# Hybrid attention and DeltaNet layer: gates projected last, two inverse groups in the merge stage, one PSUM bank for both scan chains

## The chip, the cores and the metric

One core of a Trainium2 chip runs the whole layer in one launch. The metric is the device time of that launch in microseconds (us), lower being better. TensorE (PE) multiplies matrices into PSUM, whose eight banks are shared out by the kernel; VectorE (DVE), ScalarE (ACT) and GpSimd (POOL) do the rest; SyncE (SP) issues most of the transfers.

## The reference

One layer over 1024 latent tokens of width 1024, with 256 context tokens. The mixer has two halves of width 512, fed by one input projection: neighbourhood attention with 8 heads, and a gated DeltaNet that runs over the sequence in both directions with 4 heads of 128. Each half is multiplied by a SiLU gate, and one output projection follows.

```python
na_q, na_k, na_v, na_z, g_qkv, g_z, g_b, g_a = jnp.split(h @ w_in, IN_SPLITS, axis=-1)
...
o_na = neighborhood_attention(heads(na_q), heads(na_k), heads(na_v),
                              heads(na_kc), heads(na_vc), rpb)
...
# DeltaNet, for each head and direction, over chunks of tokens
t_inv = lax.linalg.triangular_solve(eye + a, jnp.broadcast_to(eye, a.shape),
                                    left_side=True, lower=True, unit_diagonal=True)
...
def step(state, xs):
    v_new = u_n - jnp.einsum('bhcd,bhde->bhce', w_n, state)
    o_n = (jnp.einsum('bhcd,bhde->bhce', q_n, state)
           + jnp.einsum('bhij,bhje->bhie', qk_n, v_new))
    state = state * gl_n[..., None, None] + jnp.einsum('bhcd,bhce->bhde', k_n, v_new)
    return state, o_n
...
y = jnp.concatenate([o_na * jax.nn.silu(na_z), o_g * jax.nn.silu(g_z)], axis=-1) @ w_out
x = x + gate[:, None] * rmsnorm(y, g_post)
```

## The kernel before

The code names the work; a scheduler that lays it out on a modelled timeline, by priorities that the code can raise, sets the order on each engine. Engines then run their lists strictly in order, and wait on semaphores. Products that need precision are made of three matmuls, of a high and a low part.

- **Phases 0 and 2** (to about 454 us). The input is normalized into hh and hl (high and low part, latent) and chh and chl (context). For each DeltaNet head h, phase 2 runs steps named by a letter each: Q, K, V are convolutions, T and B turn queries and keys, F is `delta_front`, which makes the triangular matrices `pm` of head h - 1 and stores them. A step p takes one piece from `projections`, a generator of independent matmuls: gates (`pz`), attention's queries and keys (`pq`, `pk`), values.
- **Inverses.** Each 128-row block of `pm` is inverted in two parts. First its 32-row diagonal blocks, 320 in all, in three groups of 120, 120 and 80 partitions (`inv_groups`): the blocks are gathered in `ab_dram`, loaded as `ab`, and DVE solves them in 31 pairs of a multiply (into `tb`) and a subtract (into `vb`). The result is stored as `yd`. Groups 0 and 1 run in phase 2, group 2 in phase a2.
- **Phase a2** (about 454 to 554 us). `inv_merge`, once a head, joins the small inverses into the 128-row ones: it loads `vd` (from `yd`) and `pmf` (from `pm_dram`), transposes `vd` to `ld` on DVE, and goes in four rounds of products and evictions (tz, tu at 32 rows, tz2, tu2 at 64 rows) to `tm`, stored in `tm_dram`. What `projections` has left is laid between.
- **Phase b** (from about 554 us). Attention goes through 64 units (4 pairs of heads, 8 row tiles, 2 heads), each with products pc, pl and po. Beside it runs `delta_scan`, head by head: ten steps of two directions d = 0 and 1, each with three matmuls in a row into the bank of that direction (`pa`), read in turn by DVE (y), ACT (vn) and DVE (s, the state), and two more products into `pos`. `phase4` then makes the output products `py`, in seven and then eight banks; the last scan results go into their last piece.

The eight banks of phase b before: two for pc, two for pl, one for po, one for each direction's pa, one for pos.

Of the kernel before, what the change touches and what calls it, by code (L numbers as in the profile page):

```python
# [11 lines left out]
F32 = mybir.dt.float32  # L12
F32R = mybir.dt.float32r
# [7 lines left out]
P = 128  # L21
# [118 lines left out]
class K:  # L140
# [50 lines left out]
    def phase0(self):  # L191
# [4 lines left out]
        self.chh = self.hp.tile([P, KC, CT], F32R, name="chh")  # L196
        self.chl = self.hp.tile([P, KC, CT], F32R, name="chl")
# [330 lines left out]
    def na_proj(self, ap, ps, pairs):  # L528
        for p in pairs:
            for i in range(2):  # L530
                w = self.load_w(self.wp, 512 * i + P * p, P, f"n{'qk'[i]}{p}")
                for gr in (2, 0, 1)[1 - i:]:
                    pq = ps.tile([P, 512], F32, name=f"p{'qk'[i]}{p}_{gr}", tag="pj", bufs=3)
                    self.mm_qk(pq, w, i, gr)
                    self.qk_out(p, i, gr, pq)
                    yield
            yield from self.gate_proj(ap, ps, p, 1536 + P * p)
# [47 lines left out]
    def na_attn(self, na, ps):  # L585
# [10 lines left out]
        nxt = load(0)  # L596
        for p in range(4):
# [65 lines left out]
    def na_unit(self, ps, p, rt, ct, qk, vv, gts, mk, sums, po):  # L663
# [7 lines left out]
        for hh in range(2):  # L671
# [7 lines left out]
            pl = ps.tile([P, 512], F32, name=f"pl{p}_{u}_{hh}", tag="sl", bufs=2)  # L679
# [39 lines left out]
    def phase2(self):  # L719
        tc, nc, I = self.tc, self.nc, self.I  # L720
        ps = self.ps
        with tc.tile_pool(name="cv", bufs=1, side="right", reuse_waits="tile") as cv:
# [4 lines left out]
            self.fill, self.ready = self.projections(cv), []  # L727
# [31 lines left out]
            blocks = iter(())  # L759
            for h in range(4):  # L760
                for c in "QK":
                    step(h, c)
                    next(blocks, None)
                for _ in blocks:
                    pass
                step(h - 1, "F") if h else step(h, "G")
                if h > 1:
                    blocks = self.inv_groups((h - 2,), lambda nm, n: cv.tile([P, n], F32, name=nm, tag=nm[:2]))
                for c in "RVppTppUB":
                    step(h, c)  # L770
                    next(blocks, None)
# [6 lines left out]
    def projections(self, pool):  # L778
        for h in range(1, 4):
            yield from self.gate_proj(pool, self.ps, 4 + h, 3584 + P * h)  # L780
        yield from self.na_proj(pool, self.ps, [1])
        w = self.load_w(self.wp, [(1024, 264)], 264, "nv0", halves=4)
        for t in range(2, 12, 2):
            self.values(pool, w, 0, [t % 10, t % 10 + 1])
            yield
        self.ready.append(True)
        yield from self.na_proj(pool, self.ps, [2, 3])
# [226 lines left out]
    def inv_merge(self, g3, ps, h):  # L1014
        nc = self.nc
        pm = []
        for d in range(2):
            pool, tag = (g3, f"pm{d}") if h % 2 else (self.pf, f"kk{d}")
            pm.append(pool.tile([P, 10, P], F32, name=f"pmf{h}_{d}", tag=tag))
            nc.sync.dma_start(pm[d], self.pm_dram[h][:, d])  # L1020
        vd = g3.tile([P, 2, 10, 32], F32, name=f"vd{h}", tag="vd", bufs=2)
# [5 lines left out]
        tm = [g3.tile([P, 10, P], F32, name=f"tm{h}_{d}", tag="tm", bufs=3) for d in range(2)]  # L1027
# [7 lines left out]
        for b in range(4):  # L1035
            sl = slice(32 * b, 32 * b + 32)
            cp = nc.scalar.copy
            cp(tm[0][sl, :, sl], vd[sl, 0])
            cp(tm[1][sl, :, sl], ld[sl, 1])
            cs = slice(32 * (b % 2), 32 * (b % 2) + 32)  # L1040
            nc.scalar.copy(xo[sl, :, cs], ld[sl, 0] if b < 2 else vd[sl, 1])
        zt = g3.tile([P, 2, 10, 32], F32, name=f"zt{h}", tag="zt", bufs=1)
        for d in range(2):
            pz = ps.tile([P, 10, 32], F32, name=f"tz{h}_{d}", tag="ta", bufs=3)
            for t in range(10):
                for b in (0, 2):
                    s1, s2 = slice(32 * b, 32 * b + 32), slice(32 * b + 32, 32 * b + 64)
                    nc.tensor.matmul(pz[s2, t, :], pm[d][s1, t, s2], ld[s1, d, t, :], start=True, stop=True,
                                     tile_position=(32 * b, 32 * b + 32))
            for b in (0, 2):  # L1050
                s2 = slice(32 * b + 32, 32 * b + 64)
                nc.scalar.copy(zt[s2, d], pz[s2])
        yield
# [18 lines left out]
        for d, t0, n in parts:  # L1072
            pz = ps.tile([P, 8, 64], F32, name=f"tz2{h}_{d}{t0}", tag="ta", bufs=3)
# [18 lines left out]
    def delta_scan(self, g3, ps, h):  # L1092
# [23 lines left out]
        chain = [ps.tile([P, 512], F32, name=f"pa{h}_{d}", tag=f"pa{d}", bufs=1)[:, :P] for d in range(2)]  # L1116
# [75 lines left out]
    def phase4(self, p4, ps, last):  # L1192
# [17 lines left out]
        banks = {"sc": 2, "sl": 2, "po": 1, "pa0": 1, "pa1": 1, "os": 1}  # L1210
# [65 lines left out]
    def phase_a2(self):  # L1276
        tc, ps = self.tc, self.ps
        with tc.tile_pool(name="a2", bufs=1, side="right", reuse_waits="tile") as ap:
            ready = self.ready
            buf = lambda nm, tag, n: self.pf.tile([P, n], F32, name=f"{nm}_{tag}", tag=tag)  # L1280

            def blocks():
                vv = buf("ab", "vv", 2 * S)
                yield from self.inv_groups((2,), lambda nm, n: buf("tb2", "qh0", n) if n < S else vv[:, :S] if "ab" in nm
                                           else vv[:, S:])
                self.mk = self.pf.tile([P, MTOT], mybir.dt.bfloat16, name="mk")
                self.load(self.mk, self.I["masks"])
                while len(ready) < 4:
                    yield
                self.na_pairs = {0: self.na_load(None, 0)}  # L1290
                yield

            def merges():
                for h in range(4):
# [3 lines left out]
                    ready.append(h)  # L1298
                    yield

            pr, gens = self.fill, (blocks(), merges())
            credit = [0.0, 0.0]
            first = True
            for _ in range(3):
                next(pr)
            for _ in pr:
                for i, (g, r) in enumerate(zip(gens, (3, 3))):
                    credit[i] += r
                    while credit[i] > 0:
                        if i:  # L1310
                            with tc.high_priority(offset=200):
                                next(g, None)
                        elif first:
                            first = False
                            with tc.high_priority(offset=300):
                                next(g, None)
                        else:
                            next(g, None)
                        credit[i] -= 1
            for g in gens:  # L1320
                for _ in g:
                    pass
# [24 lines left out]
    def run(self):  # L1347
        tc = self.tc
        with ExitStack() as ctx:
# [12 lines left out]
            with tc.tile_pool(name="np", bufs=1, side="right", reuse_waits="tile") as self.np, ExitStack() as fx:  # L1362
                with tc.tile_pool(name="wp", bufs=1, side="left", reuse_waits="tile") as self.wp, \
                     tc.tile_pool(name="hp", bufs=1, side="left", reuse_waits="tile") as self.hp, \
                     tc.tile_pool(name="as", bufs=1, space=PSUM, reuse_waits="tile") as self.ps:
                    with tc.tile_pool(name="vp", bufs=1, side="right", reuse_waits="tile") as self.vp:
                        self.phase0()
                    self.phase2()
# [25 lines left out]
```

## Time and profile before

| | |
|---|---|
| Median of three runs | 905.87 us (905.06 to 906.93) |
| Profiled execution, its own time | 904.01 us |
| Its span | 902.3 us |
| Mean granted TensorE clock | 0.963 |
| Matmuls on TensorE | 6082 |

The profile is of one execution; its own time is 1.7 us more than the span that the profile shows, and 1.9 us less than the median. A row of a timeline gives start, duration, engine, line, operation, output<-input, a count where several are joined, and in brackets the idle time before it with what ended it. A row of a table by stage gives the stretch, its length, and for each engine the busy time with the number of instructions, then the granted TensorE clock, the share of DMA busy, and GB/s.

### The profile page before, as it was taken

Reading aid. Unit: us, or ns where it says so; the run is one execution under the profiler, and the core shown is the slowest. Engines: PE = TensorE matmul, PEld = TensorE weight load, DVE = VectorE, ACT = ScalarE, POOL = GpSimd, SP = SyncE. Lnnn points to the kernel's source line nnn. Section 1 sums busy time; section 2 is a strip of 40 time slices with the busy share of each in tenths; the row PEclk is TensorE's granted clock in tenths of the full one; section 3 lists DMA queues with packets and bytes.
Section 4 is the critical chain, followed back from the end, with each engine's and each line's share of the span. In section 5 each row is a group of like instructions: output and inputs, shape, how many; then the busy total and the mean of one; then the engine's idle time right before and its main releaser. Section 6 shows DMA issues by size and latency. Waiting matters only on the chain.

```text
span 902.3 us, 16602 instructions
## 1 busy us (share of the span) xinstructions
PE 848.5 (94%) x6082; PEld 708.7 (79%) x6082; DVE 537.6 (60%) x1179; ACT 416.2 (46%) x1165; POOL 369.6 (41%) x431
## 2 busy tenths in 40 slices
PE   6999999999999989998998998999999988998996
PEld 4688887887788767787887877888887876887785
DVE  3463454456545699689428634677777775662442
ACT  5262525545645445652334444555545656532310
POOL 1432322614543532455241124568557569423210
PEclk9999999999999989999998985999999998999898
DMA  9786432346355534733799699949387152132351
GB/s 343 257 290 228 150 107 74 114 157 199 89 198 185 138 122 151 216 99 112 249 265 265 219 281 413 267 117 296 141 208 272 48 183 76 47 117 94 108 183 60
DMA packets 95176, 160.98 MB, mean 178 GB/s; under 512 B 28581, under 2 KB 55542, under 8 KB 92918
## 3 DMA queue, kind: packets, MB, share of 16 engines
q1 hardware_dynamic: 87606, 146.25, 51.2%
q10 hardware_dynamic: 7488, 13.67, 4.9%
q8 instruction: 48, 0.79, 0.4%
q14 instruction: 34, 0.28, 0.1%
HBM read 110.82 MB, written 52.42 MB: 181 GB/s over the span
## 4 chain that ended last, share of the span: by engine, by line
PE 64%; DVE 13%; DMA 9%; ACT 5%; issue 4%; POOL 2%; SPq 2%; ACTq 0%; DVEq 0%; POOLq 0%
PE py L1218 3%; PE py L1219 3%; PE py L1220 3%; DVE tb L1003 3%; PE pl L688 2%; DVE vb L1006 2%; PE po L715 2%; PE pl L697 2%; PE pz L464 2%; PE pc L684 2%; PE pz L460 2%; PE pz L465 2%; PE po L710 2%; PE pa L1138 2%; PE pa L1144 2%
## 5 line engine op out<-in xcount | busy, mean ns | idle before, releaser
L676 POOL TENSOR_TENSOR gm<-gt,mk 128x288 f32<-128x288 f32 (+1 forms) x64 | 64.3, 1009 | 36.0 <-DVE nm L693 35.9
L1125 POOL TENSOR_SCALAR kd<-kt,kd 128x128 f32<-128x128 f32 x72 | 43.4, 606 | 35.3 <-PE pa L1144 33.7
L694 ACT ACTIVATE pt<-pt,nm 128x288 f32<-128x288 f32 (+1 forms) x64 | 36.7, 574 | 35.7 <-DVE nm L693 35.5
L945 ACT ACTIVATE em<-em,gc 128x128 f32<-128x128 f32 x80 | 25.5, 391 | 38.2 <-DMA em<-gc_dram 32.3
L693 DVE CUSTOM_DVE_ANT_0 pt<-pl,gm,mi 128x288 f32<-128x288 f32 (+1 forms) x64 | 36.1, 564 | 11.5 <-PE pl L688 4.9
L699 DVE COPY tl<-pl 96x384 f32<-96x384 f32 (+1 forms) x64 | 35.3, 551 | 10.2 <-PE pl L697 9.9
L692 DVE TENSOR_REDUCE mi<-pc 128x1 f32<-128x256 f32 x64 | 26.8, 420 | 22.0 <-PE pc L684 21.1
L464 PE MATMUL pz<-hl,wh_gz 128*128 128x512 f32 x96 | 38.6, 402 | 0.0
L460 PE MATMUL pz<-hh,wh_gz 128*128 128x512 f32 x96 | 38.4, 400 | 0.0
L465 PE MATMUL pz<-hh,wl_gz 128*128 128x512 f32 x96 | 38.3, 399 | 0.0
L473 PE MATMUL pv<-wh_nv,hh 128*128 128x264 f32 x128 | 35.5, 295 | 2.5 <-ACT hh L262 1.7
L964 POOL TENSOR_SCALAR_AFFINE_SELECT qe<-qe 128x256 f32<-128x256 f32 x32 | 26.9, 840 | 25.8 <-DVE qe L963 25.8
L475 PE MATMUL pv<-wl_nv,hh 128*128 128x264 f32 x128 | 35.7, 286 | 1.5 <-POOL wl_nv L446 1.5
L474 PE MATMUL pv<-wh_nv,hl 128*128 128x264 f32 x128 | 36.5, 289 | 0.0
L1003 DVE TENSOR_TENSOR tb<-ab,vb 120x31 f32<-120x31 f32 (+15 forms) x62 | 32.1, 518 | 6.8 <-DMA ab<-ab_dram 5.1
L960 DVE SCALAR_TENSOR_TENSOR pm<-pk,beta,em 128x128 f32<-128x128 f32 x80 | 23.6, 343 | 19.9 <-PE pk L953 12.3
L697 PE MATMUL pl<-c,pt 128*96 128x128 f32 (+1 forms) x192 | 33.7, 285 | 1.4 <-ACT pt L694 1.2
L812 DVE SCALAR_TENSOR_TENSOR acc_v<-xp_v,cols,acc_v 128x1282 f32<-128x1282 f32 x16 | 27.5, 1719 | 9.0 <-ACT acc_v L810 8.9
L1138 PE MATMUL pa<-y,tm 128*128 128x128 f32 x144 | 29.1, 287 | 2.8 <-DVE y L1134 2.2
L1266 ACT ACTIVATE finv<-py 128x512 f32<-128x512 f32 x16 | 9.5, 599 | 46.8 <-PE py L1220 28.3
L1128 POOL TENSOR_SCALAR vb<-v,beta 128x128 f32<-128x128 f32 x40 | 24.2, 606 | 16.7 <-DVE y L1134 10.6
L704 ACT COPY tcx<-pc 128x256 f32<-128x256 f32 x64 | 23.8, 372 | 15.3 <-PE pc L702 15.1
(438 smaller groups left out, 2928.8 us busy)
## 6 DMA issues: line engine op xcount, KB each, us to landing
wada<-in_w_ada SPq DMA_DIRECT2D x16, 512.0 KB, 9.1
em<-gc_dram SPq DMA_DIRECT2D x20, 256.0 KB, 4.6
pm_dram<-pm SPq DMA_DIRECT2D x20, 256.0 KB, 3.3
pmf<-pm_dram SPq DMA_DIRECT2D x8, 640.0 KB, 8.0
tm_dram<-tm SPq DMA_DIRECT2D x8, 640.0 KB, 7.0
kk<-qk_dram SPq DMA_DIRECT2D x16, 320.0 KB, 7.9
tm<-tm_dram SPq DMA_DIRECT2D x4, 1280.0 KB
kq_dram<-kq SPq DMA_DIRECT2D x4, 1152.0 KB
```

Of the source, the lines that this page charges most:

```text
L460: r = nc.tensor.matmul(ps, wh, xh, start=(k == 0), stop=False)
L464: nc.tensor.matmul(ps, wh, xl, start=False, stop=False)
L465: nc.tensor.matmul(ps, wl, xh, start=False, stop=(k == KC - 1))
L474: nc.tensor.matmul(ps, xl, wh, start=False, stop=False)
L475: nc.tensor.matmul(ps, xh, wl, start=False, stop=(k == KC - 1))
L676: nc.gpsimd.tensor_tensor(gm[:, :n].rearrange("p (n c r) -> p n c r", c=nco, r=4), gv, mk[:, mo:mo + n].rearrange("p (n c r) -> p n c r", ...
L693: nc.vector.tensor_tensor_reduce(pt[:, :n], pl[:, :n], gm[:, :n], -1.0, mi, ALU.add, ALU.min, nm)
L694: nc.scalar.activation(pt[:, :n], pt[:, :n], AF.Exp, bias=nm, scale=-1.0, accum_out=sums[:, ct, hh, 0:1])
L697: nc.tensor.transpose(pl[:m, rc * P:(rc + 1) * P], pt[:, rc * m:(rc + 1) * m], self.ident)
L1003: nc.vector.tensor_tensor(t3, bc(ab[:, 0:m, m:m + 1], [r, m, n]), bc(vb[:, m:m + 1, m:], [r, m, n]), ALU.mult)
L1125: nc.gpsimd.tensor_scalar(kd, kt_[:, t, :], self.kd[:, h, d, t:t + 1], None, ALU.mult)
L1138: nc.tensor.matmul(pa, tm[:, d, t, :], y, start=True, stop=True)
```

## The change

- chh and chl move to a pool of their own, xp, closed after phase 2.
- `projections` gives attention's queries, keys and values first, the key ahead of the query, and all six gate projections last.
- Inverse group 0 alone is in phase 2; groups 1 and 2 are both in phase a2, with one buffer for each of `ab`, `vb`, `tb`. The masks and the first loads of attention are issued at the start of phase a2.
- `inv_merge` loads `vd` ahead of `pmf`, from pools with other numbers of buffers (pmf three, vd one, tm four); its twelve ACT copies come behind the first products; for heads 2 and 3 the products tz and tz2 go into tag tb, with two banks.
- `delta_scan` has one bank for both directions, and the bank that is free (sx) takes every third pl from the 17th unit on.

```diff
-        self.chh = self.hp.tile([P, KC, CT], F32R, name="chh")
-        self.chl = self.hp.tile([P, KC, CT], F32R, name="chl")
+        self.chh = self.xp.tile([P, KC, CT], F32R, name="chh")
+        self.chl = self.xp.tile([P, KC, CT], F32R, name="chl")
...
+            self.nsl += 1
+            tag, nb = ("sx", 1) if self.nsl > 16 and self.nsl % 3 == 0 else ("sl", 2)
+            pl = ps.tile([P, 512], F32, name=f"pl{p}_{u}_{hh}", tag=tag, bufs=nb)
...
+                for c in "QKFRVppTppUB":
+                    if c != "F":
+                        step(h, c)
+                    else:
+                        step(h - 1, "F") if h else step(h, "G")
+                        if h == 2:
+                            blocks = self.inv_groups((0,), lambda nm, n: cv.tile([P, n], F32, name=nm, tag=nm[:2]))
+                    n += 1
+                    if n % 2:
+                        next(blocks, None)
...
     def projections(self, pool):
...
+        for p in range(1, 4):
+            yield from self.na_proj(self.ps, p)
+            if p == 1:
+                w = self.load_w(self.wp, [(1024, 264)], 264, "nv0", halves=4)
+                for ts in ((2, 3), (4, 5, 6), (7, 8, 9), (0, 1)):
+                    self.values(pool, w, 0, ts)
+                    yield
+        for j, c0 in [(4 + h, 3584 + P * h) for h in range(1, 4)] + [(p, 1536 + P * p) for p in range(1, 4)]:
+            yield from self.gate_proj(pool, self.ps, j, c0)
...
     def inv_merge(self, g3, ps, h):
...
+        ta, na = ("ta", 3) if h < 2 else ("tb", 2)
+        pm = [g3.tile([P, 10, P], F32, name=f"pmf{h}_{d}", tag="pmf", bufs=3) for d in range(2)]
+        vd = g3.tile([P, 2, 10, 32], F32, name=f"vd{h}", tag="vd", bufs=1)
...
+        tm = [g3.tile([P, 10, P], F32, name=f"tm{h}_{d}", tag="tm", bufs=4) for d in range(2)]
...
-        chain = [ps.tile([P, 512], F32, name=f"pa{h}_{d}", tag=f"pa{d}", bufs=1)[:, :P] for d in range(2)]
+        pas = ps.tile([P, 4, P], F32, name=f"pa{h}", tag="pa", bufs=1)
+        chain = [pas[:, d, :] for d in range(2)]
...
     def phase_a2(self):
...
-                vv = buf("ab", "vv", 2 * S)
-                yield from self.inv_groups((2,), lambda nm, n: buf("tb2", "qh0", n) if n < S else vv[:, :S] if "ab" in nm
-                                           else vv[:, S:])
                 self.mk = self.pf.tile([P, MTOT], mybir.dt.bfloat16, name="mk")
                 self.load(self.mk, self.I["masks"])
-                while len(ready) < 4:
-                    yield
                 self.na_pairs = {0: self.na_load(None, 0)}
-                yield
+                for g in (1, 2):
+                    yield from self.inv_groups((g,), lambda nm, n: ap.tile([P, n], F32, name=nm, tag=nm[:2]))
...
+            gens = [(merges(), 3), (blocks(), 2)]
+            for _ in self.fill:
+                for g, n in gens:
+                    with tc.high_priority(offset=200):
+                        for _ in range(n):
                             next(g, None)
...
```

How the order of instructions moves, at three places. Numbers at the end of a name tell instances apart; the first digit behind it is the head or group, and a name in brackets is the semaphore that the instruction waits for.

On DVE, at the transpose ld1 that begins merge 1. Before, it stands behind the first operations of group 2 (`ab_vv`, 80 rows), since `yd1` was there since phase 2:

```order
L1034 STREAM_TRANSPOSE ld0_4388<-vd0_4387 128x640 [waits DMAHW4_49,DMAHW5_49,DMAHW3_49,DMAHW2_49]
L1003 TENSOR_TENSOR tb2_qh0_4370<-ab_vv_4368 80x31 [waits DMAHW7_49,DMAHW1_49,Pool_49]
L1006 TENSOR_TENSOR ab_vv_4368<-ab_vv_4368,tb2_qh0_4370 80x31 [waits DVE_49]
L1003 TENSOR_TENSOR tb2_qh0_4370<-ab_vv_4368 80x60 [waits DVE_49]
L1006 TENSOR_TENSOR ab_vv_4368<-ab_vv_4368,tb2_qh0_4370 80x30x2 [waits DVE_49]
```

After, all 62 operations of group 1 (`vb1`, 120 rows) and four of group 2 (`vb2`) come ahead of it; these are the last of them:

```order
L1006 TENSOR_TENSOR tb1_4523<-ab1_4520,vb1_4522 120x31 [waits DVE_49]
L1009 TENSOR_TENSOR vb1_4522<-vb1_4522,tb1_4523 120x31 [waits DVE_49]
L1006 TENSOR_TENSOR tb2_4862<-ab2_4859,vb2_4861 80x31 [waits DMAHW2_49,DVE_49,Pool_49]
L1009 TENSOR_TENSOR vb2_4861<-vb2_4861,tb2_4862 80x31 [waits DMAHW3_49,DVE_49]
L1006 TENSOR_TENSOR tb2_4862<-ab2_4859,vb2_4861 80x60 [waits DVE_49]
L1009 TENSOR_TENSOR vb2_4861<-vb2_4861,tb2_4862 80x30x2 [waits DVE_49]
L1037 STREAM_TRANSPOSE ld1_4901<-vd1_4900 128x640 [waits DMAHW4_49,DMAHW5_49,DMAHW1_49,DMAHW0_49]
```

The second half of vd1 is read from `yd1`, so ld1 now waits for group 1's end, its store and a load.

On SP, the loads of the scan (v, kt, kq, qe, tm, zg of heads 0 and 1) stand after the change ahead of group 2's input `ab2`, of group 1's store `yd1` and of vd1:

```order
L153 DMA tm0_5788<-tm_dram0_85 128x2560 [waits DMAHW6_49,DMAHW5_49,DMAHW0_49]
L1169 DMA zg0_6615<-z_dram_95 128x1024
L153 DMA v1_6647<-vt_dram1_82 128x1280
L153 DMA kt1_6648<-kt_dram1_78 128x1280
L153 DMA kq1_6646<-kq_dram1_70 128x2304 [waits DMAHW1_49]
L983 DMA ab2_4859<-ab_dram_94 80x1024 [waits DMAHW2_49,DVE_49]
L1015 DMA yd1_4857<-vb1_4522 120x1024 [waits DMAHW3_49,DVE_49]
L1026 DMA vd1_4900<-yd1_4857 32x20x32 [waits DMAHW4_49,DMAHW3_49]
```

Before, group 2's input and both halves of vd1 stood among merge 0's loads, and none of the scan's:

```order
L1025 DMA vd0_4387<-yd0_3389 32x20x32 [waits DMAHW5_49]
...
L980 DMA ab_vv_4368<-ab_dram_94 80x1024 [waits DMAHW7_49,DMAHW0_49]
...
L1025 DMA vd1_4700<-yd0_3389 32x20x32 [waits DMAHW2_49]
L1025 DMA vd1_4700<-yd0_3389 32x20x32 [waits DMAHW3_49]
L1025 DMA vd1_4700<-yd1_4175 32x20x32 [waits DMAHW4_49]
L1025 DMA vd1_4700<-yd1_4175 32x20x32 [waits DMAHW5_49]
```

So ab2 moved from the start of phase a2 to behind the scan's first loads.

On PE, in the scan beside attention's last unit. Before, the two directions (`pa3_0` and `pa3_1`) alternate, and output products `py` follow soon:

```order
L1144 MATMUL pa3_0_8407<-vn3_0_7_8922,kd3_0_7_8917 128x128 [waits Activation_49]
L1138 MATMUL pa3_1_8408<-y3_1_4_8936,tm3_8389 128x128 [waits DVE_49]
L1133 MATMUL pa3_0_8407<-s3_0_7_8926,kq3_8386 128x128 [waits DVE_49]
L1152 MATMUL pos3_8409<-s3_0_5_8804,kq3_8386 128x128 [waits DVE_49]
L1153 MATMUL pos3_8409<-vn3_0_6_8832,qe3_8390 128x128
L1218 MATMUL py0_0_9198<-wo_qh00_8296,m3_9132 128x512 [waits PE_49,Activation_49]
```

After, behind the first output products, a stretch of 84 products of head 3's scan (51 pa, the rest pos) has no `py` in it; it begins:

```order
L1136 MATMUL pa3_8409<-s3_1_0_8509,kq3_8388 128x128 [waits DVE_49]
L1155 MATMUL pos3_8410<-s3_1_0_8509,kq3_8388 128x128 [waits DVE_49]
L1141 MATMUL pa3_8409<-y3_1_9_8588,tm3_8391 128x128 [waits DVE_49]
L1147 MATMUL pa3_8409<-vn3_1_9_8591,kd3_1_9_8584 128x128 [waits Activation_49,Pool_49]
L1156 MATMUL pos3_8410<-vn3_1_9_8591,qe3_8392 128x128
L1136 MATMUL pa3_8409<-s3_0_2_8578,kq3_8388 128x128 [waits DVE_49]
L1155 MATMUL pos3_8410<-s3_0_2_8578,kq3_8388 128x128 [waits DVE_49]
L1141 MATMUL pa3_8409<-y3_0_3_8603,tm3_8391 128x128 [waits DVE_49]
```

The three matmuls of direction 1 now stand together, and then those of direction 0. The first of each three (L1136) waits for DVE, which reads the last result of the other direction out of the shared bank.

More of the change, by code (lines that the diff above doesn't have):

```diff
@@ L759, in phase2 @@
             blocks = iter(())
+            n = 0
             for h in range(4):
[L761 to L771, printed above, removed]
+                for c in "QKFRVppTppUB":
[8 more added lines that the diff above has]
+                        next(blocks, None)
             step(3, "F")
@@ L1297, in merges @@
                     yield from self.inv_merge(ap, ps, h)
[L1298 to L1317, printed above, removed]
+            gens = [(merges(), 3), (blocks(), 2)]
[3 more added lines that the diff above has]
+                        for _ in range(n):
                             next(g, None)
-                        credit[i] -= 1
-            for g in gens:
+            for g, n in gens[::-1]:
                 for _ in g:
```

68 lines of the change are left out of this document (26 added, 42 removed).

## Prediction

> **What bounds the kernel now.** I read the page first, then busy time by stage, then the timeline around the inverses and the scan.
>
> ```profile
> span 902.3 us, 16602 instructions
> PE 848.5 (94%) x6082; PEld 708.7 (79%) x6082; DVE 537.6 (60%) x1179; ACT 416.2 (46%) x1165; POOL 369.6 (41%) x431
> PE 64%; DVE 13%; DMA 9%; ACT 5%; issue 4%; POOL 2%; SPq 2%; ACTq 0%; DVEq 0%; POOLq 0%
> ...
> core 0: us, PE busy (x) PEld busy (x) DVE busy (x) ACT busy (x) POOL busy (x), PEclk, DMA share, GB/s
> 300.00:454.00 154.00, 142.46 (x808) 121.21 (x808) 125.17 (x234) 68.10 (x185) 64.48 (x62) 0.97 0.51 155
> 454.00:554.00 100.00, 91.71 (x1340) 77.06 (x1338) 50.42 (x115) 43.30 (x95) 24.95 (x27) 0.86 0.92 277
> 554.00:790.00 236.00, 223.02 (x1921) 193.51 (x1920) 168.08 (x520) 132.07 (x484) 150.23 (x195) 0.97 0.57 176
> 790.00:836.00 46.00, 42.57 (x214) 34.96 (x214) 19.46 (x38) 14.03 (x33) 12.89 (x11) 1.00 0.31 103
> 836.00:902.00 66.00, 58.44 (x241) 46.56 (x239) 25.05 (x42) 12.75 (x35) 8.91 (x18) 0.92 0.36 120
> ```
>
> TensorE is busy 94% of the span, and 64% of the chain that ended last is its own work. The stages are: end of phase 2 (to 454), merges (to 554), attention with the scan beside it (to 790), output products with the scan's end (to 836), output products alone. In each TensorE is busy nine tenths or so: every dependent chain is laid beside independent matmuls. So the question for each edit is whether it takes work away, or the cover of a chain.
>
> **Gates last: products leave the merge stage.** Phase 2's last result (pm) is begun at 452.5, and the stage that follows still has 96 gate matmuls (pz) besides the query and key ones:
>
> ```profile
> L960 DVE SCALAR_TENSOR_TENSOR pm<-pk,beta,em x80: 340/342/353, 206.5 to 452.5; 128x128 f32<-128x128 f32 x80
> ...
> 454.00:554.00 100.00, 23.07 (x96) 17.88 (x96) 2.75 (x4) 2.39 (x4) 0.86 0.92 277
> ```
>
> By the order, 235 matmuls of 512 columns stood behind that result, and 153 stand there now. 82 move ahead, at 23.07 / 96 = 0.24 us each: 19.7 us. Phase 2 has room for some: 154.00 - 142.46 = 11.5 us of idle TensorE in its last stretch, and DVE there is freed of one inverse group. So the result comes 8 to 20 us later, at 460 to 472; I take 466. The context pool itself moves no instruction and costs nothing: what it frees is the space that the merge stage's tiles need.
>
> **Two inverse groups in the merge stage.** An inverse group is 31 multiplies and 31 subtracts on DVE, each waiting for the last. What one costs here, and what follows it:
>
> ```profile
> 465.29 0.37 SPq L980 DMA_DIRECT2D ab_vv<-ab_dram  x1
> ...
> 467.46 0.85 DVE L1034 STREAM_TRANSPOSE ld<-vd 128x640 f32<-128x640 f32 x1 [0.38 <-DMA vd<-yd]
> 472.26 0.20 DVE L1003 TENSOR_TENSOR tb_qh<-ab_vv 80x31 f32<-80x31 f32 x1 [3.96 <-DMA ab_vv<-ab_dram]
> ...
> 512.27 0.18 DVE L1006 TENSOR_TENSOR ab_vv<-ab_vv,tb_qh 80x31 f32<-80x31 f32 x1
> ...
> 528.66 0.84 DVE L1034 STREAM_TRANSPOSE ld<-vd 128x640 f32<-128x640 f32 x1 [0.37 <-ACT tm L1039]
> ...
> 554.33 0.49 DVE L1087 TENSOR_SCALAR tm<-tu 64x320 f32<-64x320 f32 x1 [0.79 <-PE tu L1084]
> ...
> 554.23 0.58 PE L684 MATMUL pc<-kk,qh 128*128 128x256 f32 x1
> ...
> 454.00:554.00 100.00, 11.37 (x31) 0.86 0.92 277
> L1003 DVE TENSOR_TENSOR tb<-ab,vb 120x31 f32<-120x31 f32 (+15 forms) x62 | 32.1, 518 | 6.8 <-DMA ab<-ab_dram 5.1
> 546.99 1.17 POOL L1031 MEMSET tm<- 128x1280 f32 x1 [0.39 <-DMA tm_dram<-tm]
> ```
>
> Group 2 runs from 472.26 to 512.27, 40 us with merges 0 and 1 between its operations. Alone its multiplies are 11.37 us and its subtracts as much: 23 us. The two groups in phase 2 took 32.1 us for the multiplies alone, so 32 us each. Then the result goes out and comes back for merge 3, whose transpose starts 16.4 us later; merge 3 ends at 554.8, 26 us on, and attention's first matmul stands right behind it.
>
> Now group 1 comes ahead of group 2 on DVE, and group 2's input waits for group 1's last read (one buffer of each). On SP's queue the scan's first loads (8 MB) are ahead of group 2's input and of group 1's store. In a row from 466:
> - loads for merge 0: before, 467.5 - 452.5 = 15 us with two stores ahead; 10 (5 to 15).
> - merge 0 up to the last negation ahead of group 1 on DVE: half of merge 3's 26 us, 13 (10 to 20).
> - group 1: between 23 and 32, 27.
> - its store, vd1 and ld1, with the scan's loads ahead: the 16.4 of before, 16 (8 to 25).
> - rest of group 2 with merges 1 and 2 between: the 40 of before (34 to 50).
> - store, vd3, ld3: 16 (8 to 20).
> - merge 3: 26, less some 6 for its second tm buffer, which was cleared only at 546.99, when a store of the one before had landed (there are four now): 20 (15 to 26). The copies that are now issued behind the first products are on ACT, off this path.
>
> 466 + 10 + 13 + 27 + 16 + 40 + 16 + 20 = 608, against 554: +54. With the low ends +9, with the high ones over +100; both sets at once are unlikely, so +25 to +75. What covered this chain before is gone: 153 matmuls are 37 us and four merges about 43, against 142 us. Attention's own loads, now early, were hidden before and gain nothing. The two banks for the last merges cost nothing that this chain doesn't hide: ACT empties a bank while DVE is in the group.
>
> **The scan in one bank.** Each step of a chain is a matmul into the bank, then a read by DVE or ACT, then the next matmul:
>
> ```profile
> 790.04 0.39 PE L1144 MATMUL pa<-vn,kd 128*128 128x128 f32 x2
> 790.47 0.35 DVE L1147 SCALAR_TENSOR_TENSOR s<-s,egl,pa 128x128 f32<-128x128 f32 x1
> 790.87 0.49 PE L1133 MATMUL pa<-s,kq 128*128 128x128 f32 x2
> ...
> L1144 PE MATMUL pa<-vn,kd x144: 270/275/421, 558.3 to 805.9; 128*128 128x128 f32 x144
> 540.00:560.00 20.00, 16.27 (x225) 15.18 (x224) 8.37 (x20) 8.18 (x23) 8.12 (x11) 0.50 1.01 414
> ...
> 554.00:790.00 236.00, 78.19 (x422) 62.42 (x423) 44.10 (x135) 23.42 (x75) 0.97 0.57 176
> 790.00:836.00 46.00, 4.88 (x26) 4.36 (x26) 3.08 (x9) 1.52 (x5) 1.00 0.31 103
> ...
> 790.00:836.00 46.00, 37.61 (x147) 26.59 (x147) 0.00 (x0) 0.00 (x0) 1.00 0.31 103
> ```
>
> From L1144's start to L1133's is 0.83 us: the step. Before, the other chain's matmul fits into it. Now each matmul of one chain waits for the read of the other, as the order shows: 240 steps that were in two chains stand in one. Of pa's records (two a step, some missing) 26 lie behind 790: 13 steps. The order has 14 behind attention's last product before, and 89 now.
>
> The Trainium skill, "PSUM — Partial Sum Buffer", section "PSUM bank collisions raise a hardware error", says that two engines may not touch the same bank and partition quadrant at once, and that a guard must go by bank, not by address. By that rule the wait can't be had away while the chains share a bank; if it did not hold, the tail below would be shorter by up to half of its 67 us of steps, 33 us. No run here shows such a collision.
>
> Of the 89, 5 lie among output products, and 84 have nothing beside them but the pos products: 84 x 0.8 = 67 us. Output products ahead of the last scan result: 162, at 37.61 / 147 = 0.256 each, 41 us. Together 108 where 46 were: +62. At the low end a step is 0.65 (0.28 for the matmul, the rest for a short read): +50. At the high end the clock is down: L1144 then takes 0.421 instead of 0.275, a step 0.95: +75. That clock is possible, since from 540 to 560 it was 0.50 with TensorE busy in 16.27 of 20 us.
>
> The Trainium skill, "TensorE: Matmul & The Clock Gate", section "What's actually happening", has the gate close after an idle window of about 3.4 us. By that rule steps of 0.8 us would keep the full clock and the tail would stay at +62; the trace speaks against it, in that 0.50 came with no more than 3.7 us idle in all of those 20.
>
> In the attention stage itself 75 steps and 37 pos products are gone:
>
> ```profile
> 789.48 0.30 PEld L1152 LDWEIGHTS pos<-s,kq 128*128 128x128 f32 x2
> 789.71 0.30 PEld L1153 LDWEIGHTS pos<-vn,qe 128*128 128x128 f32 x2
> 789.93 0.30 PEld L1144 LDWEIGHTS pa<-vn,kd 128*128 128x128 f32 x2
> ```
>
> Their pitch is 0.22 us, so 112 x 0.22 = 25 us less work. Each wait for the other chain also holds up attention's matmuls behind it, as PE takes them in order; steps come every 236 / 151 = 1.6 us there, longer than one takes, so little of that shows: I give 7 back. The third bank for every third pl can at most save the stage's idle 13 us. -18 (-38 to +10).
>
> **Sum.** 54 - 18 + 62 = +98. The profiled execution took 904.0 us around its span of 902.3; the median of the runs shown is 905.9, 1.9 more. 904.0 + 98 = 1002, on the median 1004. Where I took a term from a row of before with other work between, it can rather shrink than grow, so I say 1000.
>
> **Rivals.**
> - TensorE stays the bound (not slower). Its 6082 matmuls stay, and at 94% busy work that is only reordered would end where it did, less at most the 13 us idle in attention and the 6 of the tm buffer: 885 to 904. This decides if DVE's chain of two groups fits into the merge stage, attention starting by 554, and a chain step costs no more than a matmul, 0.28. For it: the busy share, and that phase 2 loses a group. Against it: 153 matmuls cannot cover 142 us, and the 0.83. 6 in 100.
> - The merge stage holds, the scan does not: the groups run while phase 2's products and loads still go on, near the low ends, +15. 904 + 15 - 18 + 62 = 963. For it: DVE has only 50.42 of 100 us busy there. 15 in 100.
> - The scan holds, the merge stage does not: a step overlaps more than I see, and the tail grows by 20 only. 904 + 54 - 18 + 20 = 960. For it: DVE, busy 19.46 of 46 us from 790 to 836, is free to read at once. Against it: the 0.83 has no idle reader in it either. 12 in 100.
> - All at the high ends, with the clock down in merges and tail: 904 + 75 + 10 + 75 = 1064. 9 in 100.
>
> **How the numbers follow.** Both costs as summed: 58 in 100, 965 to 1040, by taking one term at a time to its end. The range that leaves out 2 in 10 reaches down to the one-sided rivals: 945 to 1040. What a measurement can tell from no change is about 0.2%, 1.8 us. Faster only if TensorE stays the bound and the idle time goes: 0.04; same 0.02; slower 0.94.
>
> **What would show it.** Attention's first matmul near 608 instead of 554, with TensorE idle and DVE in L1006/L1009 operations before it; ld1 behind group 1; pa matmuls in the last stage one at a time, about 0.8 us apart, for some 50 us without output products between them; DMA and total busy times unchanged. It is wrong if attention starts before 570, or if the last scan result comes less than 70 us behind attention's end.

## The result, and the profile after

The changed kernel takes 1042.45 us (median of 4 runs, 1039.41 to 1044.83) against 905.54 us beside it: 1.151 times as long (95% interval 1.148 to 1.155). Forecast were 1000 us, 945 to 1040. The direction was right; the time is 42 us above the forecast and outside its range.

The page of the changed kernel: the span, busy time, the granted clock in 40 slices, and the chain that ended last.

```profile
span 1041.5 us, 16593 instructions
PE 914.4 (88%) x6082; PEld 750.6 (72%) x6082; DVE 542.7 (52%) x1179; ACT 420.8 (40%) x1165; POOL 375.0 (36%) x431
PEclk8999999999999999998855569999999956855999
PE 69%; DVE 11%; DMA 9%; ACT 5%; issue 3%; SPq 2%; POOL 1%; DVEq 0%; ACTq 0%; POOLq 0%
```

The 6082 matmuls are the same, yet TensorE is busy 66 us longer: the clock row has two holes, in the merge stage and in the scan's tail. By stage (end of phase 2, merges, attention, output products with the scan's end, output products alone):

```profile
300.00:462.00 162.00, 155.14 (x782) 126.40 (x781) 106.97 (x184) 76.81 (x200) 75.94 (x66) 0.99 0.52 165
462.00:604.00 142.00, 82.92 (x1261) 72.53 (x1260) 69.61 (x178) 39.85 (x90) 22.14 (x27) 0.65 0.71 212
604.00:832.00 228.00, 203.18 (x1679) 168.11 (x1680) 145.26 (x441) 118.95 (x428) 124.20 (x154) 0.96 0.53 152
832.00:978.00 146.00, 126.77 (x452) 96.21 (x451) 50.35 (x117) 31.21 (x89) 42.70 (x54) 0.65 0.14 51
978.00:1041.00 63.00, 55.68 (x242) 44.62 (x239) 25.24 (x42) 12.73 (x35) 8.95 (x18) 0.97 0.38 126
```

Against before the stages end 10, 50, 43, 142 and 139 us later. The merge stage took 40 us more, attention 7 less, the tail 99 more, the rest 3 less. Forecast were 54 more, 18 less, 62 more and no change.

DVE in the merge stage, and POOL's clearing of group 2's buffer:

```profile
478.45 0.84 DVE L1037 STREAM_TRANSPOSE ld<-vd 128x640 f32<-128x640 f32 x1 [10.49 <-DMA vd<-yd]
501.39 0.21 DVE L1006 TENSOR_TENSOR tb<-ab,vb 120x31 f32<-120x31 f32 x1 [3.59 <-DMA ab<-ab_dram]
...
528.36 0.19 DVE L1009 TENSOR_TENSOR vb<-vb,tb 120x31 f32<-120x31 f32 x1
543.28 0.20 DVE L1006 TENSOR_TENSOR tb<-ab,vb 80x31 f32<-80x31 f32 x1 [14.73 <-POOL vb L1000]
544.87 0.84 DVE L1037 STREAM_TRANSPOSE ld<-vd 128x640 f32<-128x640 f32 x1 [0.64 <-DMA vd<-yd]
...
579.88 0.19 DVE L1009 TENSOR_TENSOR vb<-vb,tb 80x31 f32<-80x31 f32 x1
587.02 0.85 DVE L1037 STREAM_TRANSPOSE ld<-vd 128x640 f32<-128x640 f32 x1 [6.96 <-DMA vd<-yd]
603.89 0.49 DVE L1089 TENSOR_SCALAR tm<-tu 64x320 f32<-64x320 f32 x1 [0.60 <-PE tu L1086]
...
542.09 0.95 POOL L999 MEMSET vb<- 80x1024 f32 x1 [15.97 <-DMA yd<-vb]
516.00:544.00 28.00, 0.00 (x0) 0.00 (x0) 12.08 (x36) 0.00 (x0) 7.16 (x9) 0.50 0.91 347
```

Group 1 runs from 501.39 to 528.55. Then DVE stands still until 543: POOL may clear group 2's vb only when group 1's result has left it, 16 us on. From 516 to 544 TensorE does nothing at all, while DMA moves 347 GB/s, for the most part the scan's first loads, issued from 518 on.

The scan's tail, three steps of the chain at full clock and three at half (start, duration; x2 is the two records of one matmul):

```profile
832.25 0.49 PE L1141 MATMUL pa<-y,tm 128*128 128x128 f32 x2
835.06 0.49 PE L1141 MATMUL pa<-y,tm 128*128 128x128 f32 x2
...
848.68 0.79 PE L1136 MATMUL pa<-s,kq 128*128 128x128 f32 x2
849.58 0.35 DVE L1137 SCALAR_TENSOR_TENSOR y<-pa,nsc,vb 128x128 f32<-128x128 f32 x1 [0.20 <-PE pa L1136]
850.02 0.76 PE L1141 MATMUL pa<-y,tm 128*128 128x128 f32 x2
850.87 0.27 ACT L1145 COPY vn<-pa 128x128 f32<-128x128 f32 x1 [3.54 <-PE pa L1141]
851.28 0.77 PE L1147 MATMUL pa<-vn,kd 128*128 128x128 f32 x2 [0.50 <-ACT vn L1145]
852.08 0.35 DVE L1150 SCALAR_TENSOR_TENSOR s<-s,egl,pa 128x128 f32<-128x128 f32 x1 [2.16 <-PE pa L1147]
852.48 0.79 PE L1136 MATMUL pa<-s,kq 128*128 128x128 f32 x2
...
832.00:836.00 4.00, 2.84 (x16) 1.79 (x14) 1.88 (x5) 1.00 (x3) 1.21 (x2) 1.00 0.00 0
836.00:840.00 4.00, 3.38 (x11) 2.54 (x12) 0.99 (x3) 0.73 (x2) 0.60 (x1) 0.50 0.00 0
920.00:924.00 4.00, 3.38 (x11) 2.42 (x10) 0.99 (x3) 0.73 (x2) 1.21 (x2) 0.50 0.00 0
```

From L1141 to L1141 at full clock: 2.81 us, 0.94 a step. From L1136 to L1136 at half clock: 3.80 us, 1.27 a step, 0.78 of it the matmul, which takes 0.49 at full clock. The clock falls four microseconds behind attention's last product, with nothing but the chain on TensorE, and it stays down although TensorE counts as busy in 3.38 of 4 us.

### The profile page after: what moved, and what is told of

It reads as the page before. It is cut to its first block, busy times and chain, and to the rows that moved or that the text cites. A ratio compares the mean times of both kernels' runs of the same rounds, so it can differ in the third digit from the quotient of the medians.

```text
span 1041.5 us, 16593 instructions
## 1 busy us (share of the span) xinstructions
PE 914.4 (88%) x6082; PEld 750.6 (72%) x6082; DVE 542.7 (52%) x1179; ACT 420.8 (40%) x1165; POOL 375.0 (36%) x431
## 4 chain that ended last, share of the span: by engine, by line
PE 69%; DVE 11%; DMA 9%; ACT 5%; issue 3%; SPq 2%; POOL 1%; DVEq 0%; ACTq 0%; POOLq 0%
PE py L1221 3%; PE py L1223 3%; PE py L1222 3%; PE pa L1147 3%; PE pos L1155 3%; PE pa L1136 2%; PE pa L1141 2%; DVE vb L1009 2%; DVE tb L1006 2%; PE pv L473 2%; PE pv L474 2%; PE pl L700 2%; PE pv L475 2%; DMA qh<-qk_dram 2%; PE pl L691 2%
## 5 line engine op out<-in xcount | busy, mean ns | idle before, releaser
L1147 PE MATMUL pa<-vn,kd 128*128 128x128 f32 x144 | 38.9, 359 | 20.3 <-ACT vn L1145 10.9
L1044 PE MATMUL tz<-ld,pmf 32*32 32x32 f32 x320 | 9.3, 232 | 52.5 <-DVE ld L1037 34.4
L1150 DVE SCALAR_TENSOR_TENSOR s<-s,egl,pa 128x128 f32<-128x128 f32 x64 | 22.0, 344 | 59.6 <-PE pa L1147 59.1
L1006 DVE TENSOR_TENSOR tb<-ab,vb 120x31 f32<-120x31 f32 (+23 forms) x93 | 37.1, 399 | 24.6 <-POOL vb L1000 14.7
L1147 PEld LDWEIGHTS pa<-vn,kd 128*128 128x128 f32 x144 | 27.3, 231 | 30.5 <-issue 13.0
L1044 PEld LDWEIGHTS tz<-ld,pmf 32*32 32x32 f32 x320 | 8.7, 147 | 53.5 <-DVE ld L1037 34.6
L696 DVE CUSTOM_DVE_ANT_0 pt<-pl,gm,mi 128x288 f32<-128x288 f32 (+1 forms) x64 | 35.9, 563 | 13.5 <-PE pl L691 8.3
L1136 PE MATMUL pa<-s,kq 128*128 128x128 f32 x144 | 40.1, 369 | 1.9 <-DVE s L1150 1.1
L1141 PE MATMUL pa<-y,tm 128*128 128x128 f32 x144 | 37.9, 353 | 2.1 <-DVE y L1137 2.0
L1143 ACT ACTIVATE vn<-pa,beta 128x128 f32<-128x128 f32 x40 | 14.7, 367 | 60.4 <-PE pa L1141 60.0
L1155 PE MATMUL pos<-s,kq 128*128 128x128 f32 x128 | 36.0, 371 | 2.2 <-DVE o L1163 1.9
```

Source lines behind the costliest of these rows:

```text
L1006: nc.vector.tensor_tensor(t3, bc(ab[:, 0:m, m:m + 1], [r, m, n]), bc(vb[:, m:m + 1, m:], [r, m, n]), ALU.mult)
L1136: nc.tensor.matmul(pa, kt, st[d], start=True, stop=True)
L1141: nc.tensor.matmul(pa, tm[:, d, t, :], y, start=True, stop=True)
L1147: nc.tensor.matmul(pa, kd, vn, start=True, stop=True)
L1155: nc.tensor.matmul(po[:, d, 0, :], kq[:, t + 8, :], st[d], start=True, stop=True)
```

## The experiments

All times are medians; the kernel before gave 902 to 905 us beside them.

### e1: two banks for the scan again

```diff
-        pas = ps.tile([P, 4, P], F32, name=f"pa{h}", tag="pa", bufs=1)
-        chain = [pas[:, d, :] for d in range(2)]
+        chain = [ps.tile([P, 512], F32, name=f"pa{h}_{d}", tag=f"pa{d}", bufs=1)[:, :P] for d in range(2)]
```

> The changed kernel with one PSUM bank for each direction of the scan again (and no third bank for pl). Theory A: the tail, 146 us from attention's last product to the last scan result against 47 before, is long because every step of one direction waits for the other, so that 84 steps of 1.27 us stand without output products beside them. Then the tail falls back to 45 to 60 us and the time to 945 to 960 us. Rival B: head 3's scan is late because its inputs or the merges come late, whatever the banks. Then the tail stays over 100 us and the time over 995.

952.3 us, 1.054 times before (1.051 to 1.057). Attention's last product (prt) and the last scan result (ot) by line:

```profile
L622 PE MATMUL prt<-c,rb x32: 272/273/421, 636.6 to 836.9; 128*128 128x128 f32 x32
L1184 PE MATMUL ot<-c,o x32: 272/273/418, 674.9 to 883.8; 128*128 128x128 f32 x32
```

The tail is 47 us, as before. Theory A holds: 90 of the 137 us hang on the shared bank.

### e2: the shared bank alone, in the kernel before

The opposite of e1's edit, with every third pl in the bank that is free.

> The kernel before with only the scan's part of the change: one bank for both directions, the other for every third pl. Theory A: the same tail of about 145 us, attention a few us shorter, start of attention unchanged at 554: 990 to 1005 us. Rival B (the tail comes from the later merges): tail under 90 us, time under 950.

988.9 us, 1.094 (1.090 to 1.098), a little under theory A's range. Attention ends at 777.0 and the last scan result comes at 925.0: 148 us, without any change in the merges. The shared bank costs 85 us by itself, and 90 on top of the other edits (e1). Attention begins 5 us later than before here, at 559.4, and takes 217.6 us, 17 less than before.

### e3: group 1 back in phase 2

```diff
-                        if h == 2:
-                            blocks = self.inv_groups((0,), lambda nm, n: cv.tile([P, n], F32, name=nm, tag=nm[:2]))
+                        for _ in blocks:
+                            pass
+                        if h > 1:
+                            blocks = self.inv_groups((h - 2,), lambda nm, n: cv.tile([P, n], F32, name=nm, tag=nm[:2]))
...
-                for g in (1, 2):
+                for g in (2,):
```

> The changed kernel with inverse group 1 back in phase 2, beside head 3's steps; everything else as changed. Theory A: attention starts late (603.8 against 554.2) because group 1 and its way out and back stand in a row with group 2 and merges 1 to 3; without it attention starts at 555 to 570 and the time is 1000 to 1012 us. Rival B: the start is set by the products that moved ahead, the gates that stand behind them and the loads queued in SP; then it stays above 590 and the time above 1025.

1028.9 us, 13.5 less than the changed kernel: the time is in rival B's range, the start of attention (584.8) in neither. The last result of phase 2 (pm) and attention's first product (pc):

```profile
L965 DVE SCALAR_TENSOR_TENSOR pm<-pk,beta,em x80: 336/341/352, 210.5 to 469.1; 128x128 f32<-128x128 f32 x80
L687 PE MATMUL pc<-kk,qh x64: 281/384/582, 584.8 to 808.6; 128*128 128x256 f32 x64
```

Attention starts 19 us earlier, 31 later than before. Phase 2 itself now ends at 469.1, 7 us later than without group 1. So group 1 costs the merge stage 26 us and gives phase 2 back 7, and another 31 us have other causes.

### e5 and e6: what the gates last cost

e5 has both edits of e1 and e3. e6 is the kernel before with only the new order of projections.

> The changed kernel with both of the earlier repairs: one bank for each direction, and inverse group 1 back in phase 2. Theory A (the parts add up): 952 less the 13.5 us that group 1's return gave with one bank, 935 to 942 us, attention starting at 583 to 587. What is left over the 905 of before is then from the gates last and from the queue of loads. Rival B: with two banks the later start of attention is partly made up for in attention and the tail; then 915 to 928 us.

> The kernel before with one edit: attention's queries, keys and values are projected first and all gates last. Theory A: 78 to 82 matmuls go ahead of phase 2's last result, which comes 15 to 18 us later (469 instead of 452.5), and the merge stage, whose chain (group 2, its way out and back, merge 3) took 102 us before, gives back at most 5: 913 to 922 us. Rival B: TensorE is the bound in both stages (92% busy), so what is moved ahead is missing behind: 903 to 908 us.

e5: 935.8 us, 1.034 (1.029 to 1.039). The parts add up, as in theory A, with attention starting at 583.0. e6: 924.3 us, 1.021 (1.014 to 1.028), a little over theory A's range and far above rival B's:

```profile
L961 DVE SCALAR_TENSOR_TENSOR pm<-pk,beta,em x80: 334/340/352, 210.0 to 469.7; 128x128 f32<-128x128 f32 x80
L684 PE MATMUL pc<-kk,qh x64: 276/384/583, 572.2 to 806.3; 128*128 128x256 f32 x64
```

Phase 2 ends 17 us later, and the merge stage is 102.5 us long, as it was (101.7). It gave nothing back for the matmuls that left it: TensorE was busy in 78.5 of its 102.5 us, where it was 93.4 of 101.7, and its mean granted clock fell from 0.86 to 0.73. That refutes rival B. The chain of group 2 and merge 3 is as long in all, but not in its parts: group 2 began 7 us later behind phase 2's last result, and merge 3 was 10 us shorter. DMA was busy 92% of the stage in both kernels, so that the chain alone sets its length is argued here, not shown.

### e7, e9, e10: parts of the change in the kernel before

e7 has only the context pool and the fourth tm buffer. e9 has the copies behind the products and tz, tz2 of heads 2 and 3 in tb. e10 has all of these, and attention's first loads queued behind merge 2's vd:

```diff
+                self.gate = self.vd_load
                 self.mk = self.pf.tile([P, MTOT], mybir.dt.bfloat16, name="mk")
                 self.load(self.mk, self.I["masks"])
                 self.na_pairs = {0: self.na_load(None, 0)}
+                self.gate = None
```

> The kernel before with the context inputs in a pool of their own and, in the space that this frees, four tm buffers instead of three. Theory A: the last merge no longer waits at 547 for the store of an earlier tm tile, so attention starts 3 to 6 us earlier; 899 to 903 us. Rival B: what follows (DMA at 414 GB/s, clock at 0.50) sets the start of attention anyway: within 2 us of before.

> The kernel before with two edits of the merges alone: the twelve ACT copies issued behind the first products, and tz and tz2 of heads 2 and 3 in tag tb. Theory A: in the changed kernel merge 3 took 17.4 us from its transpose to its last eviction, against 26.2 before; half of that comes from these edits, so attention starts 3 to 5 us earlier: 899 to 902 us. Rival B: merge 3 took longer before because merge 2 ran into it, and the start stays as it is: within 2 us of before.

> The kernel before with the context pool, four tm buffers, the merge edits of the run with copies, and one thing more: the masks and attention's first loads are queued behind merge 2's vd, so that the freed space can't bring them ahead of the merges. Theory A: the context pool made the kernel 1.1% slower only because attention's loads came ahead of merge 0's (its transpose at 492.8 instead of 467.5); with that taken back the edits of the merges show, attention starts at 546 to 552, and the time is 895 to 902 us. Rival B: the loads that are held back are then late for attention, or something else is behind the 1.1%: 905 us or more.

None is faster. e7: 914.4 us, 1.011 (1.008 to 1.014), neither theory's range. Attention's loads came first on SP, and merge 0's transpose 25 us later than before:

```profile
468.74 1.58 SPq L153 DMA_DIRECT2D ql<-qk_dram  x2
488.57 2.11 SPq L1025 DMA_DIRECT2D vd<-yd  x4
...
492.77 0.84 DVE L1034 STREAM_TRANSPOSE ld<-vd 128x640 f32<-128x640 f32 x1 [0.93 <-DMA vd<-yd]
```

Merge 3's transpose was then 7.5 us late (536.1 for 528.7), and attention's start 15 (569.2 for 554.2): with four tm buffers too, DVE waited 10.7 us in merge 3 for POOL to clear one. e9: 924.8 us, 1.021 (1.020 to 1.023), neither range, attention at 574.0. With three tm buffers, the copies that come later let POOL's clearing of tm wait for a store (first row), and DVE and ACT for POOL:

```profile
POOL tm L1031 <- DMA tm_dram<-tm: 28.6, 5, 18.4
...
DVE tm L1067 <- POOL tm L1031: 23.0, 2, 20.2
```

Why that store came so late was not settled. e10: 916.1 us, 1.012 (1.010 to 1.014), rival B: attention's kk, held back, was issued at 548, and attention began at 569.3. Yet merge 0's transpose was hardly earlier than in e7:

```profile
487.00 0.85 DVE L1034 STREAM_TRANSPOSE ld<-vd 128x640 f32<-128x640 f32 x1 [1.71 <-DMA vd<-yd]
```

Its vd was issued at 482.0, behind a store of attention's queries (481.6), with none of attention's loads ahead of it. So those loads are not what made merge 0 late, or not alone; why vd comes so late in both was not settled. No version faster than the kernel before came of this.

### e8, e11, e13: the stall between the groups

e8 gives each group its own vb. e11 is e5 with attention's loads behind merge 2's vd. e13 is the changed kernel with the scan's first loads behind merge 3's vd:

```diff
+            if h < 2:
+                self.gate = self.vd_load
             self.load(dst, src)
```

> The changed kernel with a vb buffer for each of the inverse groups 1 and 2 (and three tm buffers instead of four, for the space). Theory A: after group 1's last operation at 528 DVE stood still for 15 us, because group 2's vb could only be cleared when group 1's result had landed, and that store was issued behind 8 MB of the scan's loads; with a buffer of its own group 2 goes on at about 532, and attention starts 10 to 14 us earlier than 603.8, time 1028 to 1034. Rival B: the way of group 1's result to merge 1 is as long, and merges 1 to 3 set the start: less than 5 us earlier, 1037 to 1045.

> The changed kernel with two banks for the scan, group 1 in phase 2, and attention's first loads queued behind merge 2's vd. Theory A: of the 935.8 us of the run without the last edit, 10 to 12 are from attention's loads ahead of the merges and of group 2's input, the rest from the gates: 922 to 928, attention's start near 572. Rival B: the order of the loads does not matter there, since DMA has time: 933 to 938.

> The changed kernel with the scan's first loads (heads 0 and 1, 8 MB) queued behind merge 3's vd; nothing else moved by hand. Theory A: group 1's store, group 2's input and vd1 no longer share DMA with those loads; the 16 us between group 1's last operation and merge 1's transpose fall to 5 to 8, and attention starts 8 to 12 us earlier than 603.8. The scan then starts later, beside a tail that is a serial chain, so that the time gains less: 1034 to 1043. Rival B: the 16 us are the way out and back itself, or other transfers fill them; start within 3 us of 603.8, time 1043 to 1060.

e8: 1043.3 us, no change, in rival B's range. Group 2's input then came last instead: DVE waits 12.2 us for it.

```profile
DVE tb L1006 <- DMA ab<-ab_dram: 16.5, 2, 12.2
```

e11: 935.3 us, no change from e5: rival B's number, but not its reason. The wait moved to merge 3's vd, which now stood behind the scan's loads:

```profile
DVE ld L1039 <- DMA vd<-yd: 30.2, 1, 30.2
```

e13: 1032.6 us, 1.144 (1.140 to 1.148), 10 us less than the changed kernel by the medians, 7 by the ratios to the kernel before. Group 1's last operation, merge 1's transpose, and the same 28 us as above:

```profile
525.67 0.19 DVE L1009 TENSOR_TENSOR vb<-vb,tb 120x31 f32<-120x31 f32 x1
...
532.94 0.84 DVE L1037 STREAM_TRANSPOSE ld<-vd 128x640 f32<-128x640 f32 x1 [0.57 <-DMA vd<-yd]
...
516.00:544.00 28.00, 9.12 (x241) 8.75 (x243) 19.80 (x59) 7.77 (x19) 2.27 (x3) 0.50 0.29 71
```

The 16.3 us between the two are 7.1 now, with DMA at 71 GB/s instead of 347, and attention starts at 591.7, 12 us earlier. Theory A holds, with the time a little under its range: it was the scan's loads that made the way out and back long. Taking away one of two things that wait for them (e8), or the other loads (e11), only showed the next.

### e4 and e12: is it the clock?

One extra matmul, or two, behind each of head 3's chain matmuls:

```diff
                     nc.tensor.matmul(pa, kt, st[d], start=True, stop=True)
+                    if h == 3:
+                        nc.tensor.matmul(pas[:, 2:4, :], wf[:, :P], wf[:, :2 * P], start=True, stop=True)
```

> The changed kernel with one more matmul behind each of head 3's chain matmuls: 128 by 256, high-precision operands of the output weights, written to an unused part of the same bank and never read; it adds work and changes no result. Theory A: a step takes 1.27 us instead of the 0.8 of the prediction because the clock is at 0.50 there, with small matmuls only; with more columns streaming the clock goes up to 0.8 or more, and the 51 uncovered steps of head 3 take 0.85 to 1.05 us: the time falls by 10 to 20 us, to 1022 to 1032. Rival B: the step is made of waits between engines, or the clock does not follow what streams; each step then gets 0.1 to 0.25 us longer: 1047 to 1058 us, clock still near 0.5.

> The changed kernel with two extra matmuls of 128 by 256 behind each of head 3's chain matmuls instead of one, written to an unused part of the bank and never read. Theory A (the clock follows the columns that stream): the clock comes back to 1.0 early in head 3's 51 uncovered steps and stays, a step takes 1.15 to 1.25 us, and the time is 1033 to 1045. Rival B (the clock does not follow): it stays at 0.50 through them, a step takes 1.65 to 1.75 us, and the time is 1058 to 1070.

e4: 1053.1 us, 1.165 (1.148 to 1.183), from two runs that differ, 1046.5 and 1059.7. The median is in rival B's range, but in the profile, which is of the shorter run, the clock comes back in the midst of the stretch, the instructions staying the same, and that is not rival B's account. The rows by stage count only the instructions on pa:

```profile
930.00:935.00 5.00, 3.56 (x12) 2.70 (x12) 0.70 (x2) 0.27 (x1) 0.50 0.00 0
935.00:940.00 5.00, 3.00 (x14) 1.96 (x13) 1.05 (x3) 0.37 (x1) 0.85 0.00 0
940.00:945.00 5.00, 2.59 (x14) 1.81 (x14) 1.04 (x3) 0.64 (x2) 1.00 0.00 0
...
929.86 0.80 PE L1137 MATMUL pa<-s,kq 128*128 128x128 f32 x2
934.30 0.80 PE L1137 MATMUL pa<-s,kq 128*128 128x128 f32 x2
...
941.55 0.49 PE L1137 MATMUL pa<-s,kq 128*128 128x128 f32 x2 [0.22 <-DVE s L1157]
944.82 0.49 PE L1137 MATMUL pa<-s,kq 128*128 128x128 f32 x2 [0.22 <-DVE s L1157]
```

Three steps with their fill take 4.44 us at 0.50 and 3.27 at 1.00. With two fills (e12: 1046.6 us, 1.157, 1.154 to 1.159) the clock falls as well, about 907, but is back at 1.00 by 915, and three steps then take 3.60:

```profile
930.00:940.00 10.00, 7.84 (x48) 6.12 (x48) 2.97 (x9) 1.74 (x5) 2.41 (x4) 1.00 0.00 0
...
934.62 0.49 PE L1137 MATMUL pa<-s,kq 128*128 128x128 f32 x2 [0.22 <-DVE s L1160]
938.22 0.49 PE L1137 MATMUL pa<-s,kq 128*128 128x128 f32 x2 [0.22 <-DVE s L1160]
```

So 1.27 us a step with no fill at half clock, 1.20 with two fills at full clock: more work, and less time a step. Theory A's figures hold for the clock and the step. The total is a little over its range: of the steps between 907 and 915, at half clock with the fill, three took 5.06 us (907.38 to 912.44), which eats what the later ones save.

## Why the prediction was wrong, point by point

- **The scan in one bank: the mechanism was right, the size of a step was not.** 84 steps alone were forecast and stood there, 33 up to 874 and 51 from 899 on, in two stretches of 42 and 64 us. The term "84 x 0.8 = 67 us" should have been 84 x 1.27 = 107. That is 40 us more, and the 37 that the tail's growth lacked are in it (99 us, not 62); the output products took 40 us, as summed (41). Two things made the step too small. Its full-clock value was read from a single pair, 0.83, and rounded down; three steps in a row give 0.94. And the clock was taken as 1.0 for the sum, with a high end of 0.95 that took the slower matmul from one record, 0.421 for 0.275, where it has two: 0.78 for 0.49. By these figures 12 of the 40 us come from the step at full clock (0.94 for 0.8) and 28 from the clock. The scan has 224 chain products, not 240, since the first step of a direction reads no state and the last writes none; the sum did not use that count. No run shows whether the waits between the two directions are needed in one bank.
- **The rule on the clock misled.** The clock was at 0.50 for all but some ten of the uncovered steps, with TensorE busy in 3.38 of 4 us. For the same reason "total busy times unchanged" failed: 914.4 us for 848.5 with the same matmuls. The Trainium skill, "TensorE: Matmul & The Clock Gate", section "What's actually happening", lets the gate close after an idle window of some 3.4 us; no gap between the steps is over 1 us. The row of before that spoke against the rule (0.50 with 16.27 of 20 us busy) was the better guide.
- **The merge stage: sum right by luck, parts not.** Attention starts at 603.8, forecast 608. The way from phase 2's last result to it is 142 us, as summed, but loads for merge 0 took 16 (10 forecast), merge 0 up to group 1 23 (13), the rest of group 2 35 (40), its way to ld3 7 (16), merge 3 17.4 (20). Only group 1 (27) and the way to ld1 (16.3 for 16) came out; the other errors cancel. e13 shows the cause named for the way to ld1. Its size fitted by luck too: it was read from ld3 of before, with none of the scan's loads ahead, whose row names ACT's work on tm (merge 2) as the last wait, not the load. Where the load was the last wait and no such loads stood ahead, the way took 7 (ld3 here, ld1 in e13).
- **Gates last.** The result came 9.6 us later, within 8 to 20. e6 shows what it is made of: 17 us for the order of the projections, less 7 for group 1 leaving phase 2.
- **"The context pool itself moves no instruction and costs nothing" was wrong.** e7 shows 1.1% for it with the fourth tm buffer: the order on SP changes, and merge 0's transpose comes 25 us later. What in the new order does it stays open, since with attention's loads held back (e10) 20 of the 25 remain. "Attention's own loads gain nothing" held; that they cost is not shown (e11).
- **Attention.** 228.2 us against 235.0: 7 less where 18 were forecast. In e1, with all steps in it, it took 233.5. In e2 the same edit took 17 off, as forecast; why it took off less in the changed kernel was not settled.
- **The rivals.** That TensorE stays the bound is refuted by e1, e2 and e6. "All at the high ends" (1064) was nearest by number only: the tail went beyond its end, and the merge stage came out at its middle.

By the medians, from before over e6, e5 and e1 to the changed kernel: the gates last 19 (13 to 25 by e6's interval), loads and merges as changed 11, group 1 in the merge stage 17, the shared bank 90. As differences of neighbours they add up to the 137 in any case; in another order they differ, group 1 being 13.5 with one bank and the bank 85 in the kernel before. The 11 were not taken apart: by themselves in the kernel before, e7, e9 and e10 cost 11, 20 and 11.

## What to carry to other kernels

A PSUM bank that two dependent chains share makes one chain of them; count its steps behind the last independent work, and price a step from several in a row, at the clock that the trace shows where such small matmuls stand alone. Work that fills a chain's waits must not be moved ahead of it: TensorE at 92% in a stage did not mean that the stage would be shorter without that work (e6). When buffers come free earlier, look at how that changes the order of the queue, and what then stands ahead of the loads on the path.

## What was not expected of the hardware

The granted clock does not follow the share of time that TensorE counts as busy. In the changed kernel's tail it is 0.50 with 3.38 of 4 us busy in 128-column matmuls; in e12, with two more matmuls of 256 columns a step, it is 1.00 with 7.84 of 10. Part of this is the clock itself, as a matmul counts for 0.78 us at half clock and 0.49 at full. But at full clock too the share does not decide: behind 2.84 of 4 us busy the clock fell (832 to 836 in the changed kernel), and with 3.47 of 5 it stayed (940 to 945 in e4). What the gate counts, and how much is enough, is not settled: with one such matmul it stayed at 0.50 for some 30 us (907 to 937) and then rose in the profiled one of two runs, whose mean clock was 0.901; the other, 13 us longer, had 0.881.
